# Stored low halves of the projection weights, and a one-hot table built with its steps a stage apart

## The chip, the cores and the metric

The kernel runs on one core of a Trainium2 chip. The number to be told is the device time of one execution in microseconds (us), the median of several runs. The core's engines each take their own instructions in order: PE is the matmul engine (PEld its weight loads), DVE the vector engine, ACT the scalar engine, POOL the GpSimd engine, SP a queue that here only issues transfers (DMA). They wait for each other through semaphores.

## The reference, cut to what matters

One decoder block over 1024 tokens of width 1024, all in float32. First a mixing layer, whose input projection has 18 chunks of 128 columns:

```
h = rms_norm(x, norm1_g) * (1 + sc1) + sh1
b_gate, c_gate, hc, q, k, v = split(h @ w_in)
y_conv = short_conv(b_gate, c_gate, hc, conv_w)
y_attn = window_attention(rms_norm(q), rms_norm(k), v, rel_bias, sinks)
x = x + g1 * (concat(group_rms_norm(y_conv), group_rms_norm(y_attn)) @ w_out)
```

Then an expert layer. Each token has 8 heads, each head finds the best 16 of 128 x 128 experts from two lists of 128 scores, and every expert is one row of `u_tab` and one of `v_tab`:

```
h2 = rms_norm(x, norm2_g) * (1 + sc2) + sh2
q = h2 @ wq                                   # 16 chunks of 128 columns
sa, sb = q[:, :, 0] @ keys[0], q[:, :, 1] @ keys[1]
top, pos = top_k(all sums of top_k(sa, 16) and top_k(sb, 16), 16)
g = softmax(top)
x = x + g2 * sum(g * gelu(u_tab[eidx] . h2) * v_tab[eidx])
```

## The kernel before, in words

Tokens are taken in three groups of 384, 384 and 256 (`GROUPS`). For each group `front` runs 42 projections of 128 output columns: 18 with `w_in`, 8 with `w_out`, 16 with `wq`. `proj` (L260) does one: it reads the weight chunk in two halves of 256 KB (L265, tile `wraw`), lets ACT round each half to a shorter format (L268, tile `wH`), lets POOL subtract that from the original (L269, tile `wL`), and then PE adds up 24 matmuls (L272): for each of 8 input chunks high by high, high weight by low activation, low weight by high activation. All three groups read and split the same 84 halves, so L268 and L269 each run 252 times. `wraw`, `wH` and `wL` have three buffers each.

The last of a group's work is a generator, `finish_topk`, that runs beside the next group's `front`. For each block of 128 tokens it yields in small steps: `select` finds the 16 experts of each head on DVE (L595 to L668; L660 and L662 build a one-hot and multiply it by the index), and `spread` (L683 to L717) turns the choice of each token into a dense 128 x 128 table of gates. One step of `spread` serves four tokens: four one-hot rows `oi` (the pattern "APVV": one by ACT in two instructions, L703 and L704, one by POOL and two by DVE, L706), one `oj` for the four (DVE, L711), four matmuls into the PSUM tile `gps` (L714), and one copy by ACT into `stage` (L715). After eight steps `stage` (2 MB) is stored by SP (L717). Five blocks go this way, 160 steps: three of the first group, two of the second. The other three blocks are gathered row by row with indirect transfers by POOL (`gather`).

`bg(us)` hands out such steps: every background task gets credit of `us` times its rate. `proj` calls it once, ahead of its two halves. The order of the instructions on each engine is then set by the framework's scheduler, from the order of the code and its own estimate of when each is ready; so the instructions of neighbouring steps are interleaved, and each engine keeps that order on the chip.

After the three groups `dense` runs the 640 tokens of the five tables through all experts as plain matmuls (L816, L873), with the gather of the other 384 tokens beside it. Its order is that of the code.

Of the kernel before, what the change touches and what calls it, by code (L numbers as in the profile page):

```python
# [21 lines left out]
P = 128  # L22
# [52 lines left out]
def hymba_peer_kernel(ctx: ExitStack, tc: tile.TileContext, a, out: bass.AP):  # L75
# [37 lines left out]
    h2s = dram.tile([2, P, NC, DT], F32, name="h2s")  # L113
    gd = dram.tile([DT // TB, P, P, TB], F32, name="gd")
    biasd = dram.tile([P, NH, 384], F32, name="biasd")

    cond = const.tile([P, 8], F32, name="cond")
    A.activation(cond, colr("c"), AF.Silu)
# [213 lines left out]
    def front(t0, T, hs, nxt):  # L332
# [9 lines left out]
        A.copy(kc, proj(a["w_in"][4], hH, hL, T))  # L342
        qT = [tmp("y", bufs=4)[:, 0:T] for c in range(4)]
        for c in range(4):
            A.copy(qT[c], proj(a["w_in"][c], hH, hL, T))
        vT = tmp("q")
        A.copy(vT[:, 0:T], proj(a["w_in"][5], hH, hL, T))

        def conv():
            ys = []  # L350
            for cc in range(4):
                cs = tmp("q")[:, 0:T]
                A.copy(cs, proj(a["w_in"][6 + 3 * cc], hH, hL, T))
# [3 lines left out]
                V.tensor_tensor(u[:, 2:T + 2], cs, proj(a["w_in"][7 + 3 * cc], hH, hL, T), op=ALU.mult)  # L357
# [6 lines left out]
                V.tensor_tensor(y, y, proj(a["w_in"][8 + 3 * cc], hH, hL, T), op=ALU.mult)  # L364
# [123 lines left out]
            rn = norm_stats(lambda c: xchunk(c, *nxt), nxt[1]) if nxt else None  # L488
        x2T = bigt(ba, "x2T", F32)
        for c in range(NC):  # L490
            pt = proj(a["w_out"][c], mH, mL, T)
# [64 lines left out]
        for mm in range(0, 16, 2):  # L556
            qs = []
            for m in (mm, mm + 1):
                qq = tmp("q")[:, 0:T]
                A.copy(qq, proj(a["wq"][m], h2H, h2L, T))  # L560
# [30 lines left out]
            V.max_index(u[:, 8:16], v[:, 8:16], s)  # L591

    def select(va, iu):
        idf = sel.tile([P, 2 * PH, 16], BF16, name="idf")
        A.copy(idf, iu)  # L595
        va4 = va.rearrange("p (h s) k -> p h s k", s=2)
        id4 = idf.rearrange("p (h s) k -> p h s k", s=2)
        cand = sel.tile([P, PH, NCAND], F32, name="cand")
# [58 lines left out]
        for s, src in ((0, aab), (1, stb)):  # L657
# [25 lines left out]
    def spread(ti, ia, ib, g):  # L683
# [9 lines left out]
        for q in range(P // TB):  # L693
            stage = gat.tile([P, P, TB], F32, name="stage")
            for t4 in range(0, TB, 4):
                ps = gp.tile([P, 4, P], F32, name="gps")
                ois = []
                for x in range(4):
                    t = q * TB + t4 + x
                    oi = gb.tile([P, P], F32, name="oi", bufs=6)  # L700
                    who = pat[t % len(pat)]
                    if who == "A":
                        A.activation(oi, iota, AF.Abs, bias=ng[:, 0, t:t + 1])  # L703
                        A.activation(oi, oi, AF.Relu, scale=ng[:, 1, t:t + 1], bias=tr[:, 2, t:t + 1])  # L704
                    else:
                        (G if who == "P" else V).tensor_scalar(oi, iota, tr[:, 0, t:t + 1], tr[:, 2, t:t + 1],  # L706
                                                               op0=ALU.is_equal, op1=ALU.mult)
                    ois.append(oi)
                t = q * TB + t4
                oj = gb.tile([P, 4, P], F32, name="oj", bufs=2)  # L710
                V.tensor_tensor(oj, iota.unsqueeze(1).to_broadcast([P, 4, P]),  # L711
                                tr[:, 1, t:t + 4].unsqueeze(2).to_broadcast([P, 4, P]), op=ALU.is_equal)
                for x in range(4):
                    PE.matmul(ps[:, x, :], ois[x], oj[:, x, :], start=True, stop=True)  # L714
                A.copy(stage[:, :, t4:t4 + 4], ps.rearrange("p t j -> p j t"))  # L715
                yield
            nc.sync.dma_start(gd[(ti * P - DT0) // TB + q], stage)  # L717

    def gather():
        state = {"n": 0}  # L720
# [299 lines left out]
    with tc.tile_pool(name="ada", bufs=2, side="right") as ap:  # L1020
# [21 lines left out]
        table.append(add(bias_table(ap), 1.0))  # L1042
        rest.append(add(ada((2, 4, 3, 5), ap, slots), ADA_RATE, ADA0))
        hs, prev = front(*GROUPS[0], hs, nxts[0])
        for t in rest:
            drain(t)
    gbc = tc.tile_pool(name="gb", bufs=1, side="right")
# [82 lines left out]
```

## Time and profile before

| what | value |
|---|---|
| runs | 2850.66, 2853.47 and 2859.0 us, median 2853.47 |
| the profiled execution | 2857.49 us, its span from first to last instruction 2855.7 us |
| busy, share of the span | PE 95%, DVE 83%, POOL 60%, ACT 38% |
| the three groups' fronts | from the start to about 1031 us |
| table steps (`gps` matmuls) | from 378.8 to 970.9 us |
| dense stage | from about 1031 us to the end |

The profiled execution is one run under the profiler: its instruction times belong to its 2857.49 us, and a change that is worked out from them is carried over to the median of the runs. A busy share is a mean over stages with different limits, so the work below is read stage by stage. A row "X <- Y" says that X was the next instruction and that its wait ended with Y.

### The profile page before, as it was taken

Reading aid. Unit: us, or ns where it says so; the run is one execution under the profiler, and the core shown is the slowest. Engines: PE = TensorE matmul, PEld = TensorE weight load, DVE = VectorE, ACT = ScalarE, POOL = GpSimd, SP = SyncE. Lnnn points to the kernel's source line nnn. Section 1 sums busy time; section 2 is a strip of 40 time slices with the busy share of each in tenths; the row PEclk is TensorE's granted clock in tenths of the full one; section 3 lists DMA queues with packets and bytes.
Section 4 is the critical chain, followed back from the end, with each engine's and each line's share of the span. In section 5 each row is a group of like instructions: output and inputs, shape, how many; then the busy total and the mean of one; then the engine's idle time right before and its main releaser. Section 6 shows DMA issues by size and latency. Waiting matters only on the chain.

```text
span 2855.7 us, 45148 instructions
## 1 busy us (share of the span) xinstructions
PE 2700.5 (95%) x15679; PEld 2445.9 (86%) x15679; DVE 2373.4 (83%) x4845; ACT 1093.9 (38%) x2193; POOL 1721.7 (60%) x1491
## 2 busy tenths in 40 slices
PE   8899988999787889999999999999999999999998
PEld 6788978789786778889989989999989889988987
DVE  3665898877899697888988888888889888888887
ACT  2455468775586643222322222232222222222221
POOL 3444475656667744666666666666666666666661
PEclk7999999999999989999999999999999999999999
DMA  7647423464344677999999999999999999999995
GB/s 243 217 155 232 121 103 115 158 216 156 97 151 137 234 227 229 342 337 343 326 322 346 340 344 335 349 325 332 347 334 324 325 339 346 333 336 345 324 327 193
DMA packets 345157, 764.31 MB, mean 268 GB/s; under 512 B 31296, under 2 KB 130016, under 8 KB 341984
## 3 DMA queue, kind: packets, MB, share of 16 engines
q0 software_dynamic: 112320, 408.99, 39.6%
q1 hardware_dynamic: 231168, 349.81, 37.4%
q8 instruction: 123, 2.02, 0.3%
q10 hardware_dynamic: 1440, 2.62, 0.2%
q14 instruction: 106, 0.87, 0.1%
HBM read 702.06 MB, written 59.24 MB: 267 GB/s over the span
## 4 chain that ended last, share of the span: by engine, by line
PE 44%; DMA 8%; DVE 6%; issue 5%; POOL 2%; ACT 1%; SPq 0%; DVEq 0%; POOLq 0%; ACTq 0%
PE pv L873 22%; PE pa L816 21%; DMA vraw<-in_v 4%; DMA uraw<-in_uT 2%; DVE pq L768 2%; DVE vdL L860 1%; POOL rows L741 1%; ACT vdH L859 1%; DVE rows L760 1%; DMA wraw<-in_wq 1%; DMA rows<-in_v,eidx 1%; POOL uL L800 1%; DVE dacc L892 0%; DVE gw L835 0%; PE pj L272 0%
## 5 line engine op out<-in xcount | busy, mean ns | idle before, releaser
L816 PE MATMUL pa<-h,uH 128*128 128x320 f32 x4096 | 772.9, 311 | 15.2 <-ACT uH L799 6.2
L816 PEld LDWEIGHTS pa<-h,uH 128*128 128x128 f32 x4096 | 648.8, 189 | 23.1 <-ACT uH L799 7.2
L873 PE MATMUL pv<-vdH,wdH 128*128 128x512 f32 x1275 | 500.0, 392 | 18.0 <-DVE dacc L892 16.4
L269 POOL TENSOR_TENSOR wL<-wraw,wH 128x512 fp32r<-128x512 f32 x252 | 351.5, 1402 | 272.7 <-ACT wH L268 249.4
L873 PE MATMUL pv<-vdL,wdH 128*128 128x512 f32 x1275 | 497.8, 390 | 0.1
L873 PE MATMUL pv<-vdH,wdL 128*128 128x512 f32 x1275 | 496.8, 390 | 0.0
L816 PE MATMUL pa<-h,uL 128*128 128x320 f32 x2048 | 469.2, 310 | 2.3 <-POOL uL L800 2.3
L800 POOL TENSOR_TENSOR uL<-uraw,uH 128x512 fp32r<-128x512 f32 x256 | 342.4, 1338 | 163.3 <-ACT uH L799 142.7
L741 POOL DMA_INDIRECT rows<-in_u,eidx x257 | 260.8, 1015 | 157.1 <-DVE aw L760 83.2
L741 POOL DMA_INDIRECT rows<-in_v,eidx x254 | 253.7, 999 | 164.6 <-DVE pq L768 117.1
L816 PEld LDWEIGHTS pa<-h,uL 128*128 128x128 f32 x2048 | 344.6, 189 | 3.3 <-POOL uL L800 3.3
L768 DVE SCALAR_TENSOR_TENSOR pq<-rows,aw,pq 128x1024 f32<-128x1024 f32 x253 | 324.5, 1282 | 3.3 <-DMA rows<-in_v,eidx 0.8
L892 DVE TENSOR_TENSOR dacc<-dacc,pv 128x512 f32<-128x512 f32 x310 | 211.9, 684 | 134.0 <-PE pv L873 111.4
L859 ACT CAST vdH<-vraw 128x512 fp32r<-128x512 f32 x255 | 153.5, 619 | 439.0 <-DMA vraw<-in_v 366.4
L799 ACT CAST uH<-uraw 128x512 fp32r<-128x512 f32 x256 | 158.3, 619 | 418.9 <-DMA uraw<-in_uT 340.5
L760 DVE CUSTOM_DVE_ANT_0 rows<-rows,pq 128x1024 f32<-128x1024 f32 x257 | 307.5, 1212 | 12.5 <-DMA rows<-in_u,eidx 10.9
L873 PEld LDWEIGHTS pv<-vdH,wdH 128*128 128x128 f32 x1275 | 239.6, 188 | 74.9 <-DVE dacc L892 24.7
L873 PEld LDWEIGHTS pv<-vdH,wdL 128*128 128x128 f32 x1275 | 239.8, 188 | 50.9
L873 PEld LDWEIGHTS pv<-vdL,wdH 128*128 128x128 f32 x1275 | 239.8, 188 | 47.3 <-DVE vdL L860 0.5
L706 POOL TENSOR_SCALAR oi<-iota,tr 128x128 f32<-128x128 f32 x160 | 198.5, 1243 | 96.2 <-PE gps L714 88.1
L860 DVE TENSOR_TENSOR vdL<-vraw,vdH 128x512 fp32r<-128x512 f32 x255 | 192.1, 770 | 71.7 <-ACT vdH L859 66.7
L842 ACT CAST wdH<-gw 128x640 fp32r<-128x640 f32 x128 | 93.0, 728 | 377.0 <-DVE gw L835 342.4
(257 smaller groups left out, 5085.7 us busy)
## 6 DMA issues: line engine op xcount, KB each, us to landing
uraw<-in_uT SPq DMA_DIRECT2D x256, 256.0 KB
vraw<-in_v SPq DMA_DIRECT2D x255, 256.0 KB
gd<-stage SPq DMA_DIRECT2D x20, 2048.0 KB
gt<-gd SPq DMA_DIRECT2D x160, 256.0 KB
wraw<-in_w_in SPq DMA_DIRECT2D x108, 256.0 KB
wraw<-in_wq SPq DMA_DIRECT2D x96, 256.0 KB
wt<-in_w_ada SPq DMA_DIRECT2D x40, 512.0 KB
wraw<-in_w_out SPq DMA_DIRECT2D x48, 256.0 KB
```

The lines of the kernel that those rows point to most:

```text
L269: G.tensor_tensor(wL, w, wH.bitcast(F32), op=ALU.subtract)
L706: (G if who == "P" else V).tensor_scalar(oi, iota, tr[:, 0, t:t + 1], tr[:, 2, t:t + 1], op0=ALU.is_equal, op1=ALU.mult)
L741: G.indirect_dma_start(out=r, out_offset=None, in_=table, in_offset=bass.IndirectOffsetOnAxis(ap=eidx[:, ti, k:k + 1], axis=0))
L760: V.tensor_tensor_reduce(out=r, in0=r, in1=h2, op0=ALU.mult, op1=ALU.add, scale=1.0, scalar=0.0, accum_out=aw[:, k:k + 1])
L768: V.scalar_tensor_tensor(acc, r, aw[:, k:k + 1], acc, op0=ALU.mult, op1=ALU.add)
L799: A.copy(uH, raw)
L800: G.tensor_tensor(uL, raw, uH.bitcast(F32), op=ALU.subtract)
L816: PE.matmul(AT[j][:, s, 0:n], l[:, c, :], h2[r][4 * h + c][:, s * n:s * n + n], start=(h == 0 and c == 0 and k == 0), stop=(h == 1 and c = ...
L859: A.copy(vH, raw)
L860: V.tensor_tensor(vL, raw, vH.bitcast(F32), op=ALU.subtract)
L873: PE.matmul(pt, l[:, P * tt:P * tt + P], r, start=(m == 0), stop=(m == 3 * J - 1))
L892: V.tensor_tensor(dst, dst, pt, op=ALU.add)
```

## The change

- `split` takes over the loading and splitting of one half. It is called for the next half before the matmuls of a half are issued, so that a half is split half a chunk ahead of its use in the order of the code; `coming` lists all 252 halves. `wL` has four buffers.
- In the first group POOL makes `wL` as before, and `save` stores it to DRAM one half later (84 stores of 256 KB by SP). In the second and third group `wL` is not made but loaded (168 loads of 256 KB by SP).
- `bg` is called for each half with half the credit.
- `spread` is cut into `make` (the one-hots), `multiply` and `evict`, and runs `make` one step ahead of `multiply` and `evict` one step behind it. `oi` has eight buffers instead of six.
- In `select` the index tile `idf` holds every index twice side by side, made by two copies, and the multiplication (L662 before) reads it in pairs. `cand` shares the buffer of `hot1`.

```diff
-    def proj(wsrc, sH, sL, T):
-        bg(24 * T / 2400 + 0.5)
+    def save(keep):
+        while len(unsaved) > keep:
+            key, wL = unsaved.pop(0)
+            lows[key] = dram.tile([P, 4, P], F32, name="low_{}{}{}".format(*key))
+            nc.sync.dma_start(lows[key], wL.bitcast(F32))
...
+    def split():
+        nm, m, h = key = coming.pop(0)
+        w = wp.tile([P, 4, P], F32, name="wraw")
+        nc.sync.dma_start(w, a[nm][m][:, 4 * h:4 * h + 4, :])
+        wH = wp.tile([P, 4, P], F32R, name="wH")
+        wL = wp.tile([P, 4, P], F32R, name="wL", bufs=4)
+        A.copy(wH, w)
+        if key in lows:
+            nc.sync.dma_start(wL.bitcast(F32), lows[key])
+        else:
+            G.tensor_tensor(wL, w, wH.bitcast(F32), op=ALU.subtract)
+            save(1)
+            unsaved.append((key, wL))
+        ready.append((key, wH, wL))
+
+    def proj(name, m, sH, sL, T):
         pt = pj.tile([P, TM], F32, name="pj")
         for h in range(2):
-            w = wp.tile([P, 4, P], F32, name="wraw")
-            nc.sync.dma_start(w, wsrc[:, 4 * h:4 * h + 4, :])
-            wH = wp.tile([P, 4, P], F32R, name="wH")
-            wL = wp.tile([P, 4, P], F32R, name="wL")
-            A.copy(wH, w)
-            G.tensor_tensor(wL, w, wH.bitcast(F32), op=ALU.subtract)
+            if not ready:
+                split()
+            key, wH, wL = ready.pop(0)
+            if key != ("wq", 15, 1):
+                split()
+            bg(12 * T / 2400 + 0.25)
...
-        idf = sel.tile([P, 2 * PH, 16], BF16, name="idf")
-        A.copy(idf, iu)
+        idf = sel.tile([P, 2, PH * 16, 2], BF16, name="idf")
+        iu4 = iu.rearrange("p (h s) a -> p h s a", s=2)
+        for s in range(2):
+            A.copy(idf[:, s].rearrange("p (h a) y -> p h a y", h=PH),
+                   iu4[:, :, s, :].unsqueeze(3).to_broadcast([P, PH, 16, 2]))
...
-            V.tensor_tensor(hot1, hot1, id4[:, :, s, :].unsqueeze(3).to_broadcast([P, PH, 16, 16]), op=ALU.mult)
+            hk = hot1.rearrange("p h a (k y) -> p (h a) k y", y=2)
+            V.tensor_tensor(hk, hk, idf[:, s].unsqueeze(2).to_broadcast([P, PH * 16, 8, 2]), op=ALU.mult)
...
+        for k in range(-1, n + 1):
+            for step, d in ((make, 1), (multiply, 0), (evict, -1)):
+                if 0 <= k + d < n:
+                    step(k + d)
+            if 0 <= k < n:
+                yield
```

On POOL, in the first table steps of the second group, before (`wL` is the subtract, `oi` a one-hot row of a table step):

```order
L706 TENSOR_SCALAR oi<-iota,tr 128x128
L269 TENSOR_TENSOR wL<-wraw,wH 128x512
L706 TENSOR_SCALAR oi<-iota,tr 128x128 x3
L269 TENSOR_TENSOR wL<-wraw,wH 128x512
L706 TENSOR_SCALAR oi<-iota,tr 128x128 x4
L269 TENSOR_TENSOR wL<-wraw,wH 128x512
L706 TENSOR_SCALAR oi<-iota,tr 128x128 x3
L269 TENSOR_TENSOR wL<-wraw,wH 128x512 x2
```

On POOL now, from the last subtracts of the first group into the table steps of the second (`kL`, `qL` and `mc` are the attention's and the convolution's own low halves):

```order
L284 TENSOR_TENSOR wL<-wraw,wH 128x512 x45
L738 TENSOR_SCALAR oi<-iota,tr 128x128 x12
L410 TENSOR_TENSOR kL<-k,kH 128x384
L418 TENSOR_TENSOR qL<-y,qH 128x384 x4
L738 TENSOR_SCALAR oi<-iota,tr 128x128 x46
L402 TENSOR_TENSOR mc_4173<-y,mc_4172 128x384 x4
```

The subtracts that stood between the one-hot rows are gone from POOL.

On SP, around the first stores of a table (`gd<-stage`) in the second group, before:

```order
L265 DMA wraw<-in_w_in 128x512 x14
L717 DMA gd<-stage 128x4096
L265 DMA wraw<-in_w_in 128x512 x4
L717 DMA gd<-stage 128x4096
L265 DMA wraw<-in_w_in 128x512
L717 DMA gd<-stage 128x4096
```

On SP now, at the first two of these stores (`wL<-low` is a load of a stored low half):

```order
L277 DMA wraw<-in_w_in 128x512 x2
L282 DMA wL<-low_w_in_939 128x512
L758 DMA gd<-stage 128x4096
L277 DMA wraw<-in_w_in 128x512
L282 DMA wL<-low_w_in_961 128x512
L277 DMA wraw<-in_w_in 128x512
L282 DMA wL<-low_w_in_1011 128x512
L758 DMA gd<-stage 128x4096
L282 DMA wL<-low_w_in_1031 128x512
```

Loads of low halves now stand behind the table stores in SP's queue, as the loads of the weights themselves did.

On ACT, some table steps of the second group, before (`stage` is the eviction, `oi` the two instructions of a one-hot row):

```order
L715 COPY stage<-gps 128x128x4
L703 ACTIVATE oi<-iota,ng 128x128
L704 ACTIVATE oi<-oi,tr,ng 128x128
L703 ACTIVATE oi<-iota,ng 128x128
L715 COPY stage<-gps 128x128x4
L704 ACTIVATE oi<-oi,tr,ng 128x128
```

And now, in the second group too:

```order
L735 ACTIVATE oi<-iota,ng 128x128
L736 ACTIVATE oi<-oi,tr,ng 128x128
L280 CAST wH<-wraw 128x512
L735 ACTIVATE oi<-iota,ng 128x128
L736 ACTIVATE oi<-oi,tr,ng 128x128
L756 COPY stage<-gps 128x128x4 x2
```

Two one-hot rows are now made ahead of two evictions, where an eviction stood between them.

## Rows read from the trace of the kernel before

**Rows 1.** Busy time by stage: us from:to, length, each engine's busy us, granted clock, DMA.

```profile
50.00:250.00 200.00, 183.32 (x971) 158.57 (x971) 109.94 (x192) 89.23 (x200) 91.70 (x66) 0.92 0.59 190
345.00:378.00 33.00, 24.73 (x110) 22.15 (x108) 32.82 (x127) 12.92 (x29) 15.55 (x12) 0.84 0.29 81
378.00:550.00 172.00, 152.20 (x1012) 133.63 (x1012) 160.27 (x469) 133.89 (x332) 114.81 (x91) 0.99 0.34 121
550.00:720.00 170.00, 162.94 (x1020) 152.00 (x1020) 123.81 (x450) 108.02 (x241) 105.52 (x85) 0.99 0.55 185
720.00:971.00 251.00, 205.89 (x1488) 184.83 (x1487) 224.86 (x708) 170.94 (x408) 177.13 (x134) 0.96 0.42 144
971.00:1031.00 60.00, 51.87 (x408) 49.34 (x407) 39.85 (x261) 27.55 (x62) 38.98 (x32) 0.96 0.66 215
1300.00:2000.00 700.00, 696.48 (x3920) 635.34 (x3919) 613.71 (x805) 189.02 (x307) 455.14 (x418) 1.00 0.96 336
```

**Rows 2.** Waits of PE, 250 to 1031 us: us in total, times, longest.

```profile
PE pj L272 <- POOL wL L269: 18.2, 17, 5.5
PE gps L714 <- DVE oi L706: 14.3, 15, 3.3
PE gps L714 <- DVE oj L711: 8.5, 12, 1.5
PE pj L272 <- ACT wH L268: 7.9, 5, 4.1
PE gps L714 <- ACT oi L704: 6.3, 6, 2.6
PE gps L714 <- ACT stage L715: 3.9, 5, 1.7
...
PE gps L714 <- POOL oi L706: 3.8, 8, 1.0
```

**Rows 3.** Groups by line: busy us and mean ns of one, idle before.

```profile
L706 DVE TENSOR_SCALAR oi<-iota,tr 128x128 f32<-128x128 f32 x320 | 123.5, 424 | 22.9 <-PE gps L714 21.5
L711 DVE TENSOR_TENSOR oj<-iota,tr 128x512 f32<-128x512 f32 x160 | 122.4, 783 | 4.7 <-PE gps L714 2.8 <-ACT tr L690 1.4 <-issue 0.2
```

**Rows 4.** Lines L706, L711, L269: ns min/median/max of one.

```profile
L706 DVE TENSOR_SCALAR oi<-iota,tr x320: 240/340/1379, 378.5 to 968.8; 128x128 f32<-128x128 f32 x160
L706 POOL TENSOR_SCALAR oi<-iota,tr x160: 783/1230/2813, 377.4 to 968.8; 128x128 f32<-128x128 f32 x160
L711 DVE TENSOR_TENSOR oj<-iota,tr x160: 637/683/1793, 377.3 to 967.0; 128x512 f32<-128x512 f32 x160
L269 POOL TENSOR_TENSOR wL<-wraw,wH x252: 1258/1292/6322, 51.9 to 1019.3; 128x512 fp32r<-128x512 f32 x126
```

**Rows 5.** Timeline of DVE and POOL, 454 to 460 us: start, length.

```profile
454.74 1.55 DVE L706 TENSOR_SCALAR oi<-iota,tr 128x128 f32<-128x128 f32 x2
...
458.12 0.59 DVE L706 TENSOR_SCALAR oi<-iota,tr 128x128 f32<-128x128 f32 x2
...
454.43 1.52 POOL L269 TENSOR_TENSOR wL<-wraw,wH 128x512 fp32r<-128x512 f32 x1 [5.19 <-ACT wH L268]
...
458.46 1.51 POOL L706 TENSOR_SCALAR oi<-iota,tr 128x128 f32<-128x128 f32 x1 [0.62 <-PE gps L714]
```

**Rows 6.** The one-hot tile of `select`: ns min/median/max.

```profile
L662 DVE TENSOR_TENSOR hot<-hot,idf x16: 2265/2283/3369, 362.8 to 1091.6; 128x2048 bf16<-128x2048 bf16 x16
L660 DVE TENSOR_TENSOR hot<-stb,rank x8: 1200/1210/2317, 369.4 to 1088.2; 128x2048 bf16<-128x2048 bf16 x8
```

**Rows 7.** Waits of SP's queue, 250 to 1031 us.

```profile
SPq L265 <- POOL wL L269: 464.9, 182, 16.1
SPq L717 <- ACT stage L715: 59.9, 9, 19.3
SPq L717 <- ACT oi L703: 36.0, 6, 14.7
```

**Rows 8.** Chain that ended last, 971 to 1031 us: longest transfer and the next.

```profile
973.99 6.45 DMA wraw<-in_wq
...
1009.88 2.91 DMA wraw<-in_wq
```

**Rows 9.** Subtracts in the last stretch of the fronts: length, POOL busy us.

```profile
971.00:1031.00 60.00, 32.01 (x25) 0.96 0.66 215
```

More of the change, by code (lines that the diff above doesn't have):

```diff
@@ L115, in hymba_peer_kernel @@
     biasd = dram.tile([P, NH, 384], F32, name="biasd")
+    lows, unsaved = {}, []
     cond = const.tile([P, 8], F32, name="cond")
@@ L258, in ch @@
         return t[c // 4][:, c % 4, :]
-    def proj(wsrc, sH, sL, T):
-        bg(24 * T / 2400 + 0.5)
+    def save(keep):
[3 more added lines that the diff above has]
+            nc.sync.dma_start(lows[key], wL.bitcast(F32))
+    coming = [(nm, m, h) for _ in GROUPS
+              for nm, ms in (("w_in", (4, 0, 1, 2, 3, 5, *range(6, 18))), ("w_out", range(8)), ("wq", range(16)))
+              for m in ms for h in range(2)]
+    ready = []
+    def split():
[13 more added lines that the diff above has]
+    def proj(name, m, sH, sL, T):
         pt = pj.tile([P, TM], F32, name="pj")
         for h in range(2):
-            w = wp.tile([P, 4, P], F32, name="wraw")
-            nc.sync.dma_start(w, wsrc[:, 4 * h:4 * h + 4, :])
-            wH = wp.tile([P, 4, P], F32R, name="wH")
-            wL = wp.tile([P, 4, P], F32R, name="wL")
-            A.copy(wH, w)
-            G.tensor_tensor(wL, w, wH.bitcast(F32), op=ALU.subtract)
+            if not ready:
+                split()
+            key, wH, wL = ready.pop(0)
+            assert key == (name, m, h)
+            if key != ("wq", 15, 1):
+                split()
+            bg(12 * T / 2400 + 0.25)
             for c in range(4):
@@ L341, in front @@
         kc = tmp("k", bufs=1)[:, 0:T]
-        A.copy(kc, proj(a["w_in"][4], hH, hL, T))
+        A.copy(kc, proj("w_in", 4, hH, hL, T))
         qT = [tmp("y", bufs=4)[:, 0:T] for c in range(4)]
         for c in range(4):
-            A.copy(qT[c], proj(a["w_in"][c], hH, hL, T))
+            A.copy(qT[c], proj("w_in", c, hH, hL, T))
         vT = tmp("q")
-        A.copy(vT[:, 0:T], proj(a["w_in"][5], hH, hL, T))
+        A.copy(vT[:, 0:T], proj("w_in", 5, hH, hL, T))
         def conv():
@@ L352, in conv @@
                 cs = tmp("q")[:, 0:T]
-                A.copy(cs, proj(a["w_in"][6 + 3 * cc], hH, hL, T))
+                A.copy(cs, proj("w_in", 6 + 3 * cc, hH, hL, T))
                 yield
@@ L356, in conv @@
                 V.tensor_copy(u[:, 0:2], upv[:, cc, :])
-                V.tensor_tensor(u[:, 2:T + 2], cs, proj(a["w_in"][7 + 3 * cc], hH, hL, T), op=ALU.mult)
+                V.tensor_tensor(u[:, 2:T + 2], cs, proj("w_in", 7 + 3 * cc, hH, hL, T), op=ALU.mult)
                 yield
@@ L363, in conv @@
                 V.scalar_tensor_tensor(y, u[:, 2:T + 2], col("cw", 8 + cc), y, op0=ALU.mult, op1=ALU.add)
-                V.tensor_tensor(y, y, proj(a["w_in"][8 + 3 * cc], hH, hL, T), op=ALU.mult)
+                V.tensor_tensor(y, y, proj("w_in", 8 + 3 * cc, hH, hL, T), op=ALU.mult)
                 ys.append(y)
@@ L490, in front @@
         for c in range(NC):
-            pt = proj(a["w_out"][c], mH, mL, T)
+            pt = proj("w_out", c, mH, mL, T)
             V.scalar_tensor_tensor(ch(x2T, c)[:, 0:T], pt, mod[:, 16 + c:17 + c], xchunk(c, t0, T),
@@ L559, in front @@
                 qq = tmp("q")[:, 0:T]
-                A.copy(qq, proj(a["wq"][m], h2H, h2L, T))
+                A.copy(qq, proj("wq", m, h2H, h2L, T))
                 qs.append(qq)
@@ L593, in select @@
     def select(va, iu):
-        idf = sel.tile([P, 2 * PH, 16], BF16, name="idf")
-        A.copy(idf, iu)
+        idf = sel.tile([P, 2, PH * 16, 2], BF16, name="idf")
[3 more added lines that the diff above has]
+                   iu4[:, :, s, :].unsqueeze(3).to_broadcast([P, PH, 16, 2]))
         va4 = va.rearrange("p (h s) k -> p h s k", s=2)
-        id4 = idf.rearrange("p (h s) k -> p h s k", s=2)
-        cand = sel.tile([P, PH, NCAND], F32, name="cand")
+        cand = sel.tile([P, PH, NCAND], F32, name="cand", tag="hot1")
         def pairs(a0, na, nbb, st):
@@ L692, in spread @@
         A.activation(ng, tps[:, 0:3:2, :], AF.Copy, scale=-1.0)
[L693 to L715, printed above, removed]
@@ new lines, in spread, with make @@
+        n, per = P // 4, TB // 4
+        made, outs, stages = {}, {}, {}
+        def make(k):
+            ois = []
+            for x in range(4):
+                t = 4 * k + x
+                oi = gb.tile([P, P], F32, name="oi", bufs=8)
+                who = pat[t % len(pat)]
+                if who == "A":
+                    A.activation(oi, iota, AF.Abs, bias=ng[:, 0, t:t + 1])
+                    A.activation(oi, oi, AF.Relu, scale=ng[:, 1, t:t + 1], bias=tr[:, 2, t:t + 1])
+                else:
+                    (G if who == "P" else V).tensor_scalar(oi, iota, tr[:, 0, t:t + 1], tr[:, 2, t:t + 1],
+                                                           op0=ALU.is_equal, op1=ALU.mult)
+                ois.append(oi)
+            oj = gb.tile([P, 4, P], F32, name="oj", bufs=2)
+            V.tensor_tensor(oj, iota.unsqueeze(1).to_broadcast([P, 4, P]),
+                            tr[:, 1, 4 * k:4 * k + 4].unsqueeze(2).to_broadcast([P, 4, P]), op=ALU.is_equal)
+            made[k] = ois, oj
@@ new lines, in multiply, with evict @@
+        def multiply(k):
+            ps = outs[k] = gp.tile([P, 4, P], F32, name="gps")
+            ois, oj = made.pop(k)
+            for x in range(4):
+                PE.matmul(ps[:, x, :], ois[x], oj[:, x, :], start=True, stop=True)
+        def evict(k):
+            q, r = divmod(k, per)
+            if r == 0:
+                stages[q] = gat.tile([P, P, TB], F32, name="stage")
+            A.copy(stages[q][:, :, 4 * r:4 * r + 4], outs.pop(k).rearrange("p t j -> p j t"))
+            if r == per - 1:
+                nc.sync.dma_start(gd[(ti * P - DT0) // TB + q], stages.pop(q))
@@ L716, in spread @@
+        for k in range(-1, n + 1):
[3 more added lines that the diff above has]
+            if 0 <= k < n:
                 yield
-            nc.sync.dma_start(gd[(ti * P - DT0) // TB + q], stage)
     def gather():
@@ L1044, in hymba_peer_kernel @@
         hs, prev = front(*GROUPS[0], hs, nxts[0])
+        save(0)
         for t in rest:
```

## The prediction

> **What bounds the kernel now.** I first cut the span into stages [rows 1]. In the dense stage PE is busy 696.48 of 700 us, and nothing in the change touches its order, so about 1825 us after 1031 us stay as they are and only the fronts can give. There PE is not alone. In the two stretches with table steps, 378 to 550 and 720 to 971 us, DVE is busy 160.27 of 172 and 224.86 of 251 us (93 and 90%), more than PE (88 and 82%). PE is idle 19.8, 7.1, 45.1 and 8.1 us in the four stretches from 378 to 1031 us, and 8.3 us from 345 to 378: 88 us in all. Read who it waits for [rows 2]: the matmuls of the table wait 14.3 + 8.5 + 6.3 + 3.9 + 3.8 = 36.8 us for their one-hot rows and evictions, the projections 18.2 us for POOL's low half and 7.9 us for ACT's high half. These 62.9 us are what the change aims at; the rest are waits of the attention, the norms and the first dense steps.
>
> Why is DVE late? Line by line, the mean of one `oi` on DVE is 424 ns and its median 340, that of `oj` 783 against 683 [rows 3, 4]. The excess is 320 x 84 ns = 26.9 us and 160 x 100 ns = 16.0 us, together 43 us on the instructions that PE waits for. It comes in a few long ones (1379 and 1793 ns at most), and the timeline shows what lies beside one: a pair of `oi` takes 1.55 us while POOL does a subtract, and 0.59 us while POOL does an `oi` of its own [rows 5]. So I take it that the subtract holds DVE up and POOL's one-hot row does not. One pair of rows is a thin basis, which is why a rival below rests on the opposite.
>
> **The change part by part.** *Subtracts that go.* 168 of 252, at a median of 1292 ns [rows 4], are 217 us of POOL. POOL is off the path as an engine (177.13 of 251 us at its fullest [rows 1]); the worth lies in three other places. First, DVE gets back up to 43 us on the table steps, all of them being in the second and third group. Second, PE's 18.2 us behind `wL` end with a load instead. Third, SP waited 464.9 us in all for POOL to free the weight buffers [rows 7]; now ACT's rounding alone frees them, so weights can come earlier.
>
> *One-hot rows a step ahead, evictions a step late, eight `oi` buffers.* No work is added: 160 steps with the same instructions. ACT no longer stands at an eviction that PE has not finished while the next one-hot row lies behind it, and PE no longer waits for an eviction just issued. `oj` still has two buffers, so nothing can run more than a step ahead, which limits the gain.
>
> These two go together into term A, the 36.8 us of table waits. 14.3 + 8.5 = 22.8 us of them are for DVE, which gets 43 us back: I take two thirds, 15 us. Of the other 14 us, for ACT and POOL, I take a third, 5 us. A = -20 us, with ends of 0 (DVE is late for other reasons) and -37.
>
> Term B, the waits on weights, 18.2 + 7.9 = 26.1 us: splitting a half ahead and loading should remove most, but a load can be late too. B = -17, with ends of -26 and, if the loads come no earlier than the subtracts did, 0. A loss is the second rival.
>
> Term C, the clock. From 720 to 971 us the granted clock is 0.96 of 2.4 GHz [rows 1]; at two levels, that is 2 x 0.04 x 251 = 20 us at 1.2 GHz, of which half, 10 us, is lost where PE works; 345 to 378 us, at 0.84, adds 5. It is granted low there and not in the stretch of 550 to 720 us (0.99), where PE is idle 7 us. If the long waits go, part of it comes back. C = -5, ends 0 and -15.
>
> *Pairs of indices.* The product with the index (16 instructions, median 2283 ns) reads one index for 16 elements; the comparison on the same shape, whose operands run through neighbouring elements, takes 1210 ns [rows 6]. With pairs I take the lower: 1.07 us less each, 12 of them in the fronts. The bounds are 0 and 1.07. The Trainium skill ("VectorE: DVE Perf Modes", What auto-detection actually checks) has the doubled rate for 16-bit tensors whose step is 1, which a pair meets; no row here shows a run as short as two. From 345 to 378 us DVE is busy 32.82 of 33 us [rows 1], so there the two products of one block count in full. D = -2; the others give DVE slack that A already counts. The second copy of `idf` is on ACT, which is busy 12.92 of those 33 us and hides it. `cand` in the buffer of `hot1` is written and read by DVE alone, in order, and costs nothing.
>
> *Transfers that come.* 84 stores and 168 loads of 0.262 MB. The dense stage moves 336 GB/s at a DMA share of 0.96 [rows 1], so one costs about 0.78 us of all engines. In the first group 84 x 0.78 = 66 us stand against 200 x 0.41 = 82 us free from 50 to 250 us alone, more up to 345. SP's stores wait for a subtract that the next weight buffer waits for as well. E1 = +1, ends 0 and +8. From 378 to 971 us the share is 0.34 to 0.55 and there is room. From 971 to 1031 us there is hardly any: 25 halves are split there [rows 9], 25 x 0.78 = 19.5 us, against 60 x 0.34 = 20.4 us free. A weight already took up to 6.45 us on the chain there, where another took 2.91 [rows 8]. E2 = +3, ends 0 and +10.
>
> Credit in two portions for a half each leaves the sum of steps as it was, and I cost it at nothing: the steps are still 160 and lie in the same stretches. Should finer steps interleave worse, A's upper end covers it.
>
> The sum: -20 - 17 - 5 - 2 + 1 + 3 = -40 us, from 2857.49 to 2817.5 us for an execution like the profiled one. That one is 4.0 us above the median of the runs, 2853.47, so I forecast 2813.5, rounded to 2814 us. Ends added up: the strongest gain is 37 + 26 + 15 + 2 = 80 us, to 2773; the weakest, A to D at zero and the transfers at their worst, is 18 us slower, 2871.
>
> **The rivals.** *The relief is small.* POOL keeps its 160 one-hot rows, and by their own numbers they do collide with something: 783 ns at best, 1230 in the median [rows 4]. If DVE is held up by any POOL work, or if the ends of ACT and DVE set the step anyway, A shrinks to -4, B to -6 as loads replace subtracts, C to 0: -4 - 6 - 2 + 4 = -8, 2845 us, and 2838 to 2856 around it. For it: half of POOL's work in the stretches stays. Against it: the 0.59 us pair beside an `oi` of POOL. The Trainium skill ("SBUF — State Buffer", Who interferes with whom) supports this rival: DVE instructions with two SBUF inputs or in a two-port mode share a port pair with any GpSimd instruction that reads SBUF, and whichever starts first keeps it to its end. The pair of 0.59 us disagrees with that, the pair of 1.55 us agrees.
>
> *The loads come late (slower).* SP issues in order. 20 table stores stand in its queue, each waiting for an eviction; together with the one-hot rows in front of it, ACT held them 59.9 + 36.0 = 95.9 us [rows 7]. Now the eviction is a step later, and a step is 591 us / 160 = 3.7 us (the `oi` from 377.4 to 968.8 us [rows 4]). Before, a held-up queue delayed a weight that had three buffers of cover; now it delays high and low half alike. If half of the 20 stores make PE wait a whole step, 10 x 3.7 = +37 us, B is lost, and A, C, D, E stay: 37 - 20 - 5 - 2 + 4 = +14, 2867 us. It decides where a low half is issued less than the 2.9 to 6.5 us of a landing [rows 8] before its first matmul. Against it: in the new order the loads behind a table store belong to halves that come some table steps and at least a dozen matmuls after the store's own step on PE.
>
> *Nearly all waits go.* without the 43 us DVE is busy 342 of 423 us (81%) in the two table stretches, and PE runs through: A -37, B -24, C -10, D -2 and the transfers hidden, -73, 2780 us. For it: 43 us and more of slack on DVE. Against it: the same engines still feed PE in order, and ACT makes three instructions a step.
>
> **How the numbers follow.** The forecast, gains of 20 to 55 us, gets 0.60; the small relief 0.18; late loads 0.10; nearly all waits gone 0.12. A measurement of this kernel tells about 0.3% from no change, 8.6 us either way. Faster than 2845: all of the forecast and the last rival, and a third of the small relief, taken down a little: 0.76. Within: 0.15. Slower: 0.09. For 8 in 10 the range leaves out late loads and the strongest gains: 2780 to 2852 us.
>
> **What would show it.** Right: no POOL subtract after the first group; mean `oi` and `oj` on DVE near 340 and 683 ns; the table matmuls' waits for DVE below 10 us; the product with the index near 1.2 us; the dense stage starting some 40 us earlier and lasting as long. Wrong: PE waiting for DMA of `wL`, a DMA share near 1 that stretches the last 60 us of the fronts, or DVE means that stay although the subtracts are gone.

## The result and the profile after

| | before | after |
|---|---|---|
| median of the runs shown with the result | 2856.23 us | 2817.57 us |
| profiled execution | 2857.49 us | 2812.93 us |
| span | 2855.7 us | 2811.2 us |

The ratio of the times is 0.9863, with a 95% interval of 0.984 to 0.9887: 38.7 us by the medians. 2814 us were forecast, with 2780 to 2852 us as the range.

The stages after, read as in [rows 1]. The stretches are cut where the same work lies now, so they begin and end elsewhere: the turn to the second group, its table steps and projections, the third group's table steps, the last projections, and a piece of the dense stage.

```profile
50.00:250.00 200.00, 179.86 (x946) 153.01 (x945) 108.03 (x190) 85.84 (x194) 92.77 (x67) 0.94 0.77 259
...
367.00:530.00 163.00, 156.46 (x1076) 140.99 (x1074) 152.07 (x513) 139.39 (x350) 71.12 (x68) 1.00 0.54 192
530.00:696.00 166.00, 159.09 (x1006) 150.59 (x1006) 114.30 (x448) 107.02 (x239) 33.82 (x37) 0.98 0.75 253
696.00:916.00 220.00, 195.42 (x1496) 181.81 (x1495) 186.92 (x706) 170.96 (x412) 70.55 (x75) 0.97 0.68 234
916.00:970.00 54.00, 48.48 (x384) 46.54 (x383) 30.77 (x207) 23.75 (x54) 3.51 (x4) 0.97 0.93 323
1300.00:2000.00 700.00, 697.28 (x3933) 636.85 (x3932) 610.30 (x782) 188.40 (x306) 452.49 (x420) 1.00 0.96 337
```

POOL has some 71 us of work in each of the two table stretches (367 to 530 and 696 to 916 us), where it had 115 and 177. PE is now the busiest engine in all of them but is still idle 24.6 us from 696 to 916 us. From 1300 to 2000 us the dense stage is as full as it was.

Where the groups ended is read from the first and the last high-by-high matmul of `wq` in each group. Before, and then after (count, ns, first to last start):

```profile
L272 PE MATMUL pj<-h2H,wH x128: 331/336/632, 252.4 to 334.7; 128*128 128x384 f32 x128
L272 PE MATMUL pj<-h2H,wH x128: 331/336/522, 618.0 to 723.6; 128*128 128x384 f32 x128
L272 PE MATMUL pj<-h2H,wH x128: 276/279/387, 948.4 to 1021.6; 128*128 128x256 f32 x128
```

```profile
L301 PE MATMUL pj<-h2H,wH x128: 332/336/632, 257.2 to 343.6; 128*128 128x384 f32 x128
L301 PE MATMUL pj<-h2H,wH x128: 332/336/522, 594.1 to 699.1; 128*128 128x384 f32 x128
L301 PE MATMUL pj<-h2H,wH x128: 276/279/522, 894.0 to 968.5; 128*128 128x256 f32 x128
```

The first group ends 8.9 us later (334.7 to 343.6). The second takes 355.5 us instead of 388.9, the third 269.4 instead of 298.0: 33.4 and 28.6 us less. At the end of the fronts that is 53.1 us; 44.5 of them are left at the end of the span, because the dense stage takes 8.6 us longer (1842.7 us from the last of these matmuls to the end, 1834.1 before). In its first 278.4 us the granted clock is 0.94 where it was 0.96, an estimate of 0.02 x 278 = 6 of these 8.6 us; why it is lower was not looked into.

PE in the second and third group together, before and then after:

```profile
334.70:1021.60 686.90, 602.80 (x4071) 548.04 (x4070) 582.50 (x2027) 454.57 (x1073) 452.86 (x351) 0.97 0.45 152
```

```profile
343.60:968.50 624.90, 579.55 (x4071) 539.62 (x4070) 505.86 (x2019) 452.86 (x1079) 179.00 (x184) 0.98 0.69 237
```

With the same number of matmuls PE is idle for 45.3 us instead of 84.1, 38.8 of the 62.0 us that the two groups lose. The other 23.2 us are shorter busy time.

What PE waited for from 250 to 1000 us, to be held against [rows 2]:

```profile
PE gps L750 <- ACT stage L756: 12.6, 9, 3.6
PE pj L301 <- ACT wH L280: 9.4, 7, 4.0
...
PE pj L301 <- DMA wL<-low_wq: 3.0, 3, 1.9
...
PE gps L750 <- DVE oj L742: 2.1, 4, 0.7
...
PE pj L301 <- DMA wL<-low_w_out: 1.3, 1, 1.3
PE pj L301 <- DMA wL<-low_w_in: 1.3, 1, 1.3
```

The 22.8 us behind DVE's one-hot rows are 2.4 (0.3 of them behind `oi`). The 18.2 us behind POOL's low halves are 5.6 behind loads of them. Among the waits of the fronts, those for ACT are the largest that are left.

DVE's and POOL's table instructions, and the product with the index (count, ns minimum/median/maximum), against [rows 4] and [rows 6]:

```profile
L738 DVE TENSOR_SCALAR oi<-iota,tr x320: 250/344/1146, 375.1 to 912.0; 128x128 f32<-128x128 f32 x160
L738 POOL TENSOR_SCALAR oi<-iota,tr x160: 785/846/1970, 374.5 to 911.4; 128x128 f32<-128x128 f32 x160
L742 DVE TENSOR_TENSOR oj<-iota,tr x160: 666/682/1487, 374.5 to 912.2; 128x512 f32<-128x512 f32 x160
...
L694 DVE TENSOR_TENSOR hot<-hot,idf x16: 1210/1222/1232, 365.8 to 1040.6; 128x2048 bf16<-128x2048 bf16 x16
```

And the means (busy us, mean ns), against [rows 3]:

```profile
L742 DVE TENSOR_TENSOR oj<-iota,tr 128x512 f32<-128x512 f32 x160 | 111.6, 703 | 13.2 <-PE gps L750 12.3 <-ACT tr L722 0.6
L738 DVE TENSOR_SCALAR oi<-iota,tr 128x128 f32<-128x128 f32 x320 | 105.6, 368 | 28.5 <-PE gps L750 27.2
```

The medians on DVE are what they were; the means fell from 424 to 368 and from 783 to 703 ns. So it is the few long ones that went. Counted over the whole trace of the kernel before, each DVE instruction assigned to the POOL instruction that it overlaps most, 31 `oi` lie beside a subtract and take 1034 ns in the mean, 228 lie beside a one-hot row of POOL and take 354; of the `oj`, 26 beside a subtract take 1168 ns and 125 beside a one-hot row 691. So the one pair of rows that the prediction went by [rows 5] is typical of this trace.

Twelve more kernels follow. A ratio is the time of a kernel over that of the kernel before, measured beside it, with its 95% interval in brackets.

### The profile page after: what moved, and what is told of

Same layout as the page of the kernel before. It is cut to its first block, busy times and chain, and to the rows that moved or that the text cites. A ratio compares the mean times of both kernels' runs of the same rounds, so it can differ in the third digit from the quotient of the medians.

```text
span 2811.2 us, 45327 instructions
## 1 busy us (share of the span) xinstructions
PE 2684.1 (95%) x15679; PEld 2443.0 (87%) x15679; DVE 2287.5 (81%) x4845; ACT 1090.8 (39%) x2201; POOL 1439.0 (51%) x1323
## 3 DMA queue, kind: packets, MB, share of 16 engines
q1 hardware_dynamic: 267456, 415.89, 44.6%
## 4 chain that ended last, share of the span: by engine, by line
PE 67%; DVE 13%; DMA 10%; issue 5%; ACT 3%; POOL 2%; SPq 0%; DVEq 0%; ACTq 0%; POOLq 0%
PE pv L921 25%; PE pa L864 23%; PE pj L301 10%; DMA vraw<-in_v 4%; PE gps L750 4%; DMA wraw<-in_wq 2%; DVE pq L816 1%; DVE vdL L908 1%; DVE rows L808 1%; PE pj L310 1%; PE po L477 1%; PE pm L195 1%; DMA rows<-in_u,eidx 1%; DVE gw L883 1%; DMA wt<-in_w_ada 1%
## 5 line engine op out<-in xcount | busy, mean ns | idle before, releaser
L738 POOL TENSOR_SCALAR oi<-iota,tr 128x128 f32<-128x128 f32 x160 | 156.0, 976 | 386.1 <-PE gps L750 203.5
L808 DVE CUSTOM_DVE_ANT_0 rows<-rows,pq 128x1024 f32<-128x1024 f32 x257 | 307.8, 1214 | 11.8 <-issue 8.8
L280 ACT CAST wH<-wraw 128x512 fp32r<-128x512 f32 x252 | 154.2, 618 | 161.5 <-PE pj L301 74.8
```

Of the source, the lines that this page charges most:

```text
L808: V.tensor_tensor_reduce(out=r, in0=r, in1=h2, op0=ALU.mult, op1=ALU.add, scale=1.0, scalar=0.0, accum_out=aw[:, k:k + 1])
```

## The experiments

**The parts alone and undone.** Theory K: POOL's subtract holds up DVE's one-hot rows. Rival S: the order of the table steps makes the gain.

*Only the stored low halves* (only_store), in the kernel before, with the fourth buffer of `wL` and `cand` in the buffer of `hot1`:

```
             A.copy(wH, w)
-            G.tensor_tensor(wL, w, wH.bitcast(F32), op=ALU.subtract)
+            if key in lows:
+                nc.sync.dma_start(wL.bitcast(F32), lows[key])
+            else:
+                G.tensor_tensor(wL, w, wH.bitcast(F32), op=ALU.subtract)
+                save(1)
+                unsaved.append((key, wL))
```

> The kernel before with one part of the change: the low halves are stored in the first group and loaded in the second and third (wL with four buffers), split where they are used; table steps, pairs and credit as before. Theory K (POOL's subtract holds up DVE's one-hot rows): the mean of oi on DVE falls from 424 to under 360 ns and of oj from 783 to under 700, PE's waits for the table rows from 36.8 to about 20 us, and the time by 20 to 30 us, to 2826 to 2836. Rival S (the order of the table steps makes the gain): only waits on weights go, at most 10 us, 2846 or more.

2818.68 us, ratio 0.9852 (0.9831 to 0.9873): by itself as much as the whole change gained, and 7 us more than K expected at most. The means on DVE are 361 and 699 ns, with the table steps in their old order:

```profile
L726 DVE TENSOR_TENSOR oj<-iota,tr 128x512 f32<-128x512 f32 x160 | 109.0, 699 | 5.5 <-PE gps L729 4.1 <-ACT tr L705 0.3
L721 DVE TENSOR_SCALAR oi<-iota,tr 128x128 f32<-128x128 f32 x320 | 102.9, 361 | 33.6 <-PE gps L729 31.6 <-ACT h2H L316 0.2
```

*Only the staged table steps* (only_stage): the new `spread` (`make` a step ahead, `evict` a step late, `bufs=8` for `oi`) in the kernel before, nothing else.

> The kernel before with one part of the change: one-hot rows made a step ahead, evictions a step late, eight oi buffers; POOL subtracts in all three groups. Theory K: DVE's means stay near 424 and 783 ns and the time falls by 0 to 8 us, 2848 to 2856. Rival S: the table's waits on PE fall from 36.8 to about 15 us although DVE's means stay, and the time falls by 20 us or more, to 2836 or less.

2865.26 us, ratio 1.0021 (1.0006 to 1.0036): no gain, if anything a small loss. S is out. The staging does shorten PE's waits for the table, from 36.8 to 26.8 us, and `oj`'s mean falls to 718 ns (`oi` is at 449). But PE waits 22.7 us for the low halves, where it waited 17.2 in this stretch before, and the granted clock from 345 to 970 us is 0.93, where the kernel before has 0.97. The rows are the waits of PE from 345 to 1031 us, then that stretch of the kernel before, then of this one, with columns as in [rows 1].

```profile
PE pj L272 <- POOL wL L269: 22.7, 22, 5.5
PE gps L718 <- DVE oj L710: 14.0, 15, 2.5
```

```profile
345.00:970.00 625.00, 544.76 (x3615) 491.61 (x3614) 541.75 (x1751) 425.76 (x1008) 412.13 (x319) 0.97 0.43 146
```

```profile
345.00:970.00 625.00, 548.93 (x3541) 501.96 (x3540) 529.79 (x1740) 417.17 (x993) 384.10 (x312) 0.93 0.41 145
```

*The change without the stored low halves* (undo_store): `split` always subtracts.

```
-        if key in lows:
-            nc.sync.dma_start(wL.bitcast(F32), lows[key])
-        else:
-            G.tensor_tensor(wL, w, wH.bitcast(F32), op=ALU.subtract)
-            save(1)
-            unsaved.append((key, wL))
+        G.tensor_tensor(wL, w, wH.bitcast(F32), op=ALU.subtract)
```

> The changed kernel without the stored low halves: POOL subtracts in all three groups, everything else as changed (split ahead, staged table steps, pairs). Theory K: DVE's means go back to about 420 and 780 ns, and 20 to 30 us of the gain are lost: 2838 to 2848. Rival S: 5 to 10 us are lost at most, 2823 to 2828.

2857.93 us, ratio 1.0004 (0.9992 to 1.0017): all of the gain is lost, 10 us more than K had, though `wL` keeps its fourth buffer. DVE's means are back at 442 and 745 ns. Splitting ahead, the staged steps and the pairs are together worth nothing while POOL subtracts.

*The change without the staged steps* (undo_stage): the old `spread` in the changed kernel.

> The changed kernel with the table steps as before (one-hot rows, matmuls and eviction of one step together, six oi buffers), low halves stored, split ahead, pairs. Theory K: DVE's means stay near 344 and 690 ns, and 5 to 10 us are lost: 2823 to 2828. Rival S: 20 us or more are lost, 2838 or more.

2819.5 us, ratio 0.9856 (0.983 to 0.9883), where the whole change has 0.9863. No loss shows, though intervals of some 7 us either way do not exclude the 5 us that K left to the staging. PE's waits for the table are 21.0 us here and 15.0 in the changed kernel.

**The hold-up by itself.** Two kernels give POOL extra work in place of the subtract; each has one of the two lines, and its name stands behind it.

```
             nc.sync.dma_start(wL.bitcast(F32), lows[key])
+            G.tensor_tensor(back[:, 0:4, :], back[:, 0:4, :], back[:, 0:4, :], op=ALU.mult)    # dummy_two
+            G.tensor_scalar(back[:, 0:4, :], back[:, 0:4, :], 1.0, None, op0=ALU.mult)         # dummy_one
```

> The changed kernel, and beside each of the 168 loads of a low half POOL multiplies a constant 128x512 tile of zeros and ones with itself: the same size and the same two inputs as the subtract, and no projection waits for it. It is added work and changes no result. Theory K1 (the subtract costs by holding up DVE): the means of oi and oj on DVE go from 344 and 690 back towards 420 and 770 ns, the stretched DVE time in the table stretches back to some 50 us, and 15 to 30 us are lost, 2833 to 2848. Rival W (the subtract costs because the projections and SP's loads wait for it): nothing waits for this one, so the time stays at 2815 to 2824, whatever DVE's means do.

> As the kernel before in this call, but POOL's added instruction has one input: the same tile times 1.0, 128x512. Theory K1 in the form that only POOL's two-input instructions hold DVE up: DVE's means stay within 360 and 710 ns, and at most 6 us are lost, 2817 to 2824. Rival (any POOL work of this size does it): means and time as with two inputs, 2833 to 2848. The Trainium skill (SBUF — State Buffer, Who interferes with whom) stands with the rival, since it names any GpSimd instruction that reads SBUF.

2957.95 us (ratio 1.0344, 1.0322 to 1.0365) and 3017.09 us (1.0562, 1.054 to 1.0585): both far outside everything expected. As tests of the time they failed. Nothing held the extra instructions back until a weight was there, so they stood bunched in front of POOL's own one-hot rows (with one input up to 25 in a row), and PE waited for those. The first row is from two inputs, the second from one:

```profile
PE gps L751 <- POOL oi L739: 55.4, 18, 15.5
```

```profile
PE gps L751 <- POOL oi L739: 126.5, 25, 27.8
```

What they do tell is DVE's means. Two inputs, 1140 ns an instruction:

```profile
L739 DVE TENSOR_SCALAR oi<-iota,tr 128x128 f32<-128x128 f32 x320 | 137.0, 464 | 80.7 <-PE gps L751 79.5
L743 DVE TENSOR_TENSOR oj<-iota,tr 128x512 f32<-128x512 f32 x160 | 117.8, 742 | 16.1 <-PE gps L751 15.1 <-ACT tr L723 0.6
L283 POOL TENSOR_TENSOR back<-back 128x512 f32<-128x512 f32 x168 | 191.6, 1140 | 9.6 <-PE pj L357 0.4
```

One input, 1544 ns an instruction:

```profile
L739 DVE TENSOR_SCALAR oi<-iota,tr 128x128 f32<-128x128 f32 x320 | 113.8, 392 | 171.2 <-PE gps L751 169.4
L743 DVE TENSOR_TENSOR oj<-iota,tr 128x512 f32<-128x512 f32 x160 | 110.7, 697 | 19.9 <-PE gps L751 18.9 <-ACT tr L723 0.6
L283 POOL TENSOR_SCALAR back<-back 128x512 f32<-128x512 f32 x168 | 259.3, 1544 | 9.8
```

259.3 us of POOL with one input lengthen `oi` to 392 ns and leave `oj` alone; 191.6 us with two inputs lengthen them to 464 and 742.

The next pair puts the extra instruction where the subtract was in the code: it works in place on the loaded weights, waits for ACT's rounding like the subtract and holds the weight buffer like it. PE takes the loaded low half and never waits for it. In the two traces POOL, DVE, ACT and PE each run the same instructions in the same order; what differs is the number of inputs, and that only the instruction with two inputs also holds the buffer of `wH`. Again each kernel has one of the two lines (together, the shadow kernels).

```
             nc.sync.dma_start(wL.bitcast(F32), lows[key])
+            G.tensor_tensor(w, w, wH.bitcast(F32), op=ALU.subtract)    # shadow_two
+            G.tensor_scalar(w, w, 2.0, None, op0=ALU.mult)             # shadow_one
```

> The changed kernel, and behind each of the 168 loads of a low half POOL subtracts the high half from the weights in place, as the subtract before did; nothing reads the result, since the matmuls take the loaded low half. POOL's work, its order among the one-hot rows and the release of the weight buffers are those of the subtract, only PE's wait for it is gone. Theory K1 (the hold-up of DVE): oi and oj on DVE go back to 420 to 450 and 740 to 780 ns, and 20 us or more of the gain are lost, 2837 to 2857. Rival W (PE's waits for the low half, 18 us before): the gain stays, 2815 to 2825. Half of each would be 2826 to 2836.

> The same, but the instruction that POOL does in place has one input (weights times 2.0, unread by anyone). By the added instruction of the last call it takes 1.54 us against 1.14 with two inputs, so POOL's queue is fuller than with shadow_two. Theory K1 in the form that two inputs hold DVE up: DVE's means stay within 380 and 710 ns, and the time is shorter than shadow_two's by 10 us or more although POOL works longer. Rival Q (POOL's one-hot rows come late behind the other instruction): as long as shadow_two or longer.

With two inputs 2882.3 us, ratio 1.0099 (1.0077 to 1.0121); with one input 2855.43 us, ratio 0.9984 (0.997 to 0.9998). By the medians 65 and 38 us more than the changed kernel, though no projection waits for POOL. Rival W, that the gain was PE's own wait for the low half, is out. The 65 us are not the price of the subtract alone: shadow_two is 24 us longer than undo_store, which makes the same subtracts but neither stores nor loads low halves. The subtracts cost 40 us there (2857.93 against 2817.57). Two inputs:

```profile
L739 DVE TENSOR_SCALAR oi<-iota,tr 128x128 f32<-128x128 f32 x320 | 130.8, 448 | 33.7 <-PE gps L751 31.9 <-ACT tr L723 1.1
L743 DVE TENSOR_TENSOR oj<-iota,tr 128x512 f32<-128x512 f32 x160 | 117.6, 742 | 9.6 <-PE gps L751 7.5 <-ACT tr L723 1.6
L283 POOL TENSOR_TENSOR wraw<-wraw,wH 128x512 f32<-128x512 f32 x168 | 235.8, 1409 | 160.8 <-ACT wH L280 159.6
PE gps L751 <- DVE oj L743: 14.5, 16, 1.9
```

One input:

```profile
L743 DVE TENSOR_TENSOR oj<-iota,tr 128x512 f32<-128x512 f32 x160 | 112.1, 707 | 13.2 <-PE gps L751 8.8 <-ACT tr L723 4.1
L739 DVE TENSOR_SCALAR oi<-iota,tr 128x128 f32<-128x128 f32 x320 | 111.9, 396 | 39.0 <-PE gps L751 36.7 <-ACT tr L723 1.4
L283 POOL TENSOR_SCALAR wraw<-wraw 128x512 f32<-128x512 f32 x168 | 271.1, 1621 | 128.5 <-ACT wH L280 125.1 <-POOL wraw L283 2.9
PE gps L751 <- DVE oj L743: 7.1, 10, 1.8
```

The instruction with one input takes longer (1621 against 1409 ns) and costs 27 us less. PE's waits say where: from 250 to 1050 us all its waits for DVE, of the table and of everything else, come to 49.6 us with two inputs and 15.9 with one, while its waits for `wH` are 9.0 and 13.3, so it is not the buffer of `wH`. So some 27 of the 65 us are the hold-up of DVE by a second input, and Q is out for that part. The other 38 were not taken apart. POOL's queue is little of it: PE waits 4.2 us for POOL's one-hot rows with one input, 0.4 with two. What is left are the weight buffers that POOL holds again, the rest of the hold-up (396 against 368 ns for `oi`) and the clock. SP's queue in the stretch from 345 to 1031 us, with one input and then after the change:

```profile
SPq L277 <- POOL wraw L283: 261.4, 133, 8.1
```

```profile
SPq L277 <- ACT wH L280: 65.5, 47, 6.0
```

**Splitting a half ahead.** The changed kernel without the early `split` (undo_ahead):

```
             key, wH, wL = ready.pop(0)
-            if key != ("wq", 15, 1):
-                split()
             bg(12 * T / 2400 + 0.25)
```

> The changed kernel with each half split where it is used instead of a half ahead; low halves stored, table steps staged, pairs, credit in two portions. Theory K: the waits of PE on weights are 20 to 26 us with or without it, and the time stays within 6 us, 2812 to 2824. Rival L (splitting ahead hides the loads): PE waits 10 us or more longer for wL and wH, 2828 or more.

2805.5 us, ratio 0.9808 (0.9783 to 0.9832), below the interval of the changed kernel. Both sides missed: I had put the splitting into term B as part of a gain, and it costs some 12 us by the medians. PE's waits on weights are 6.3 us for `wH` here and 9.4 with the splitting ahead. From 345 to 1031 us SP's weight loads wait 61.4 us for ACT's rounding to free a buffer here and 65.5 with the splitting ahead, its loads of low halves 189.5 and 196.8 us for PE: in both kernels a load goes out when a buffer comes free, so splitting earlier in the code has little to bring. What the 12 us are made of was not settled; the two profiled executions show only 4.1 of them (2807.1 against 2811.2 us), 3.2 by the end of the first group. This version is the fastest that was run.

**The pairs.** The kernel before with stored low halves and pairs (store_pairs): `select` as changed, in the kernel of the first experiment.

> The kernel before with stored low halves and the pairs of indices; table steps, splitting and credit as before. By only_store (2818.7) and the pairs' 16 x 1.07 us, of which I put 2 on the path: 2812 to 2819. If the pairs do more because DVE sets the pace of the table stretches: 2805 to 2811.

2821.09 us, ratio 0.9867 (0.9846 to 0.9888), where the stored halves alone have 0.9852. 16 products went from 2285 to about 1220 ns, 17 us of DVE, and the time does not show it. That fits PE's waits in only_store, where DVE's one-hot rows are 3.4 us in all: once the subtracts were gone, PE hardly waited for DVE in the table steps.

**POOL's rows, and the stores.** Two tries at more. The first, hot_ppvv, gives ACT's one-hot row to POOL:

```
-HOT = "APVV"
+HOT = "PPVV"
```

> The changed kernel with the one-hot rows' pattern PPVV for APVV: POOL makes two of four rows, ACT none. After the change PE waits longest in the table steps for ACT (12.6 us for the eviction), and POOL is free of the subtracts. Theory K with rows only on POOL: 160 x (0.40 + 0.49) = 142 us leave ACT, 160 x 0.98 = 156 us come to POOL, PE's waits for the eviction fall to some 4 us, and the time by 5 to 12 us, to 2806 to 2813. Rival (POOL's rows hold DVE up too, or POOL's two rows of a step, 2 us, come late): the time stays or grows by up to 10 us, 2817 to 2828.

2861.17 us, ratio 1.0012 (0.9993 to 1.0031): the gain is gone, 33 us worse than the worst that I had allowed. Not by DVE, whose means are 367 and 700 ns with twice the rows on POOL. PE waits for POOL's rows, 28.6 of the 44 us by which it is longer than the changed kernel; the rest was not traced:

```profile
PE gps L750 <- POOL oi L738: 28.6, 58, 1.3
```

So one-hot rows on POOL, which have one tensor input, do not hold DVE up, as the first pair of timeline rows had suggested [rows 5].

The second, stores_by_act, lets ACT issue the stores of the low halves,

```
-            nc.sync.dma_start(lows[key], wL.bitcast(F32))
+            A.dma_start(lows[key], wL.bitcast(F32))
```

in the kernel without splitting ahead:

> undo_ahead (2805.5: the change without splitting a half ahead) with the 84 stores of low halves issued by ACT's queue instead of SP's. The first group took 9 us longer with the change (its end 345 against 336 us in the profiles). If that is SP holding weight loads behind stores that wait for a subtract, it comes back: 2796 to 2802. If it is the transfers themselves, nothing changes, 2803 to 2808; if ACT, waiting for a subtract in its queue, delays its own roundings, 2809 or more.

2822.63 us, ratio 0.988 (0.986 to 0.9899): 17 us worse, the third of the expected cases. The first group ends at 354.0 us, in undo_ahead at 340.4, and ACT's roundings now stand behind stores that wait for POOL (this wait is 2.5 us in undo_ahead):

```profile
ACT wH L280 <- POOL wL L284: 44.4, 20, 6.7
```

What the 9 us in the first group are stays open between SP's order and the transfers. ACT's waits up to 345 us in the changed kernel at least name the transfers (2.6 us for `wq` and 7.5 for `w_out` before):

```profile
ACT wH L280 <- DMA wraw<-in_wq: 21.8, 12, 5.0
ACT wH L280 <- DMA wraw<-in_w_out: 13.0, 7, 3.3
```

## Why the prediction was right, point by point

*The stage and the size.* The gain is in the fronts, as forecast, and the sum of -40 us met -38.7 by the medians (-44.6 from one profiled execution to the other). That it met so closely is in part luck, by two misses that cancel. The fronts got 53.1 us shorter in the profiles, where the terms as measured below come to about -29; and the dense stage, which was to last as long as before, gave 8.6 us back. (The profiled execution is also 4.6 us faster than the median of its runs.) What the terms miss is in PE's busy time, which they did not count beyond the clock: 23.2 us less in the second and third group. The clock is some 7 of these. A wait that is shorter than the matmul before it shows as busy time, not as idle: table matmuls start 112 ns apart in the median and take 275. Added up from each start to the next, PE spent 185.7 us on the tile `gps` before and 153.5 after, 32 us less, where its idle time there tells of 22.

*Term A, -20 us for the table's waits.* Measured: 36.8 us became 15.0 (12.6 for evictions, 2.4 for DVE's rows), -22. The reason given first, DVE held up by the subtract, is shown by the runs: the means follow POOL's two-input instructions in and out of the kernels (358 to 368 and 691 to 706 ns without them in the table steps, 424 to 464 and 718 to 783 with them). The reason given beside it, the staged steps, shows in PE's waits and not in the time: they take 10 us off the table's waits alone and 6 beside the stored halves, but alone they gave no time, and without them no loss shows. I had taken a wait that goes for time that goes.

*Term B, -17 us for the waits on weights.* 26.1 us became 15.0 (9.4 for `wH`, 5.6 for loads), -11. shadow_two shows that the subtract's price does not lie in this wait: the instruction costs more than the whole gain where no projection waits for it. The prediction named SP's loads that wait for POOL to free a buffer and gave them no term; the runs show these waits come and go with POOL's work (412.7 us from 345 to 1031 us before, 244.5 and 261.4 in the shadow kernels, none after the change) but not what they cost. And splitting ahead belonged in the sum with the other sign.

*Term C, -5 us for the clock.* From 345 to 970 us the granted clock went from 0.97 to 0.98, an estimate of 0.01 x 625 = 6 us; read in 50 slices of 12.5 us it is 0.970 and 0.981, 7 us. The size holds. It is also a price that the experiments pay: 0.95 with shadow_two, so by the same estimate 0.03 x 625 = 19 of its 65 us.

```profile
345.00:970.00 625.00, 544.39 (x3606) 500.67 (x3605) 541.85 (x1829) 422.68 (x1007) 376.37 (x315) 0.95 0.60 206
```

*Term D, -2 us for the pairs.* The instruction came out near the lower of the two durations that I had weighed, at 1222 ns. On the path its worth is too small to tell from 0: the intervals of only_store and store_pairs are some 6 us either way.

*Term E1, +1 us for the stores, ends 0 and +8.* The first group takes 8.9 us longer, just beyond the upper end (5.6 to 9.4 in undo_ahead, store_pairs and only_store). I had compared the transfers with the free share of 200 us and found room; but the DMA share of 0.59 became 0.77, and weights came later although the engines were not full: up to 345 us PE waits 11.8 us for `wH` and `wL`, where it waited 5.3. A mean share did not tell when a transfer lands.

*Term E2, +3 us for the last stretch.* The projections of `wq` in the third group take 74.5 us instead of 73.2 at a DMA share of 0.93. The size holds.

*The rivals.* The small relief is out: POOL's one-hot rows go on and hardly hold DVE up. The Trainium skill's rule ("SBUF — State Buffer", Who interferes with whom), by which a DVE instruction with two SBUF inputs contends with a GpSimd instruction that reads SBUF, fits the two-input instructions here and not the one-input ones, which at 1544 ns left `oj` at 697 ns; the measurement decides. Late loads did not come either: PE waits 5.6 us for low halves in all.

## What to carry to other kernels

An engine that is off the critical path can still cost time through what it shares: compare the mean of a short instruction with its median, and look in the timeline at what lies beside the long ones. When several edits aim at one wait, run each alone before sharing out the gain. Work that runs ahead in the code has little to bring where loads already go out as soon as a buffer comes free. And when a sum meets the measurement, check its terms one by one: here two misses cancelled.

## What was not expected of the hardware

- DVE instructions are lengthened by POOL instructions with two tensor inputs and hardly by those with one: `oj` has a mean of 742 ns in the kernels with 168 two-input instructions and 697 to 707 with as many longer one-input ones. `oi` feels one input too, though less: assigned by overlap as above, the 38 beside the added instruction take 1048 ns in the mean in shadow_two, the 75 in shadow_one 475.
- POOL's rows are lengthened too, whether or not it subtracts: its `oi` takes 1299 ns in the mean in only_store, where the subtracts are gone from the table steps, and 785 at least in the changed kernel. With the steps staged they get shorter: 976 in the changed kernel, 1240 in undo_stage. The shorter rows on POOL gave no time, and what lengthens them was not tested.
- In only_stage PE's idle time in the second and third group is 82 us, where the kernel before has 84, and yet the granted clock of the 625 us fell from 0.97 to 0.93, by estimate 25 us if PE worked all that time. What lowered it is not shown.
